# Moving the last pair of x's sums and two pooled differences by one step, and two bias copies to ScalarE, in a one-core hybrid decoder layer

## The chip, the core and the metric

The kernel runs on one core of one Trainium2 chip. The core has five engines, each with its own queue of instructions, which it works off in order: TensorE (PE; its weight loads are listed apart as PEld) multiplies matrices into PSUM banks, VectorE (DVE) and ScalarE (ACT) work element by element on SBUF tiles and PSUM banks, GpSimd (POOL) works on SBUF tiles, and SyncE (SP) issues most of the DMA transfers. The engines wait for each other by semaphores.

The metric is the time of one execution in microseconds (us), the median of several runs. The profile shows one more execution, instruction by instruction.

## The reference

One layer over 512 positions of width 1024, all in float32. Cut to what matters here:

```python
u = rmsnorm(x, ln1_g[i])
proj = u @ w_in[i]
q, k, v, pool_in, z, xbc, dt_raw, gate_pre = jnp.split(proj, split_idx, axis=-1)
y_a = dilated_attention_mixer(q, k, v, rel_bias) @ w_a[i]
y_b = pool_mixer(pool_in, pool_w[i], pool_scale[i]) @ w_b[i]
y_c = ssd_mixer(z, xbc, dt_raw, ...) @ w_c[i]
merged = gates[:, :, 0] * y_a + gates[:, :, 1] * y_b + gates[:, :, 2] * y_c
x = x + merged @ w_o[i]
x = x + conv_ffn(rmsnorm(x, ln2_g[i]), ...)
return rmsnorm(x, final_g)
```

Two of its parts matter for the change. The pool mixer takes, for each of four groups of 256 channels, the mean over the last w = 2, 4, 8 or 16 positions, less the channel itself:

```python
outs.append((c - shifted) / cnt - uf[..., sl])
```

The attention adds to its scores a bias, looked up in a table of 32 buckets per head by the distance of query and key.

## The kernel before

**Products in three parts.** A float32 product is computed from split operands. A weight block (a "job", with its own number n) is fetched into a tile raw, cast into a high part wh by ScalarE (`cast`, L200) and left with a low part wl = raw - wh by VectorE (`lows`, L220). `u` lies in SBUF, turned, as high part uh and low part ul. Each product is then high x high, high x low and low x high (`mm3`, L239), in this order, so that the low part wl is needed last. Buffers are few: two tiles wl, three wh, two raw. A low part can therefore only be written when TensorE has left the job two before it.

**Order of the jobs at the start.** Four jobs of pool channels (eight blocks m = 0 to 7 of 128 channels; the first two jobs are written out by hand in `begin`, L1872), then two jobs of v (n = 4 and 5, each with four row blocks, matmuls pb), then two sets of products for the first queries and keys, interleaved (n = 6 to 19, matmuls p), then the pool mixer's own product (n = 20, matmuls ppw). While job n is multiplied, the low part of n+1 and the cast of n+2 are issued ahead of its matmuls (`prepare`).

**Sets of seven.** Each set computes a 2 x 2 block product with seven products instead of eight (`sevens`), named one to seven. The operands are quarters of the weights and of u, or sums of such quarters. The weights' sums are made in place by `plus` (L354) on VectorE and by accumulating DMAs that GpSimd issues (L375). The sums of u are made by `sums_of_u(p)` for the pairs p = 0 to 3, as a generator in four stages, one a step: (A) two sums uf = uh + ul on VectorE (L390); (B) four half sums into sa and sb on VectorE (L329 to L332); (C) their high parts sah and sbh on ScalarE (L335, L336); (D) their low parts sal and sbl on VectorE (L338, L339). Job five (n = 8) is the first that reads them.

**Steps.** The side work runs in generators on a list `running`. After a certain number of matmuls the kernel calls `step()`, which advances every generator by one stage, in the order of the list. The steps that matter: steps 1 to 8 follow the pool blocks m = 0 to 7, steps 9 and 10 lie in v's first job (after two and after four row blocks), 11 and 12 in its second, and from 13 on there is one step after every second job of the sets (13 after n = 7, 14 after n = 9, 15 after n = 11, 16 after n = 13). `after(n, it)` waits n steps before the first stage. Line 1942 starts the pairs with waits of 0, 0, 5 and 6 steps. So pair 2 has its stages A to D in steps 6 to 9, pair 3 in steps 7 to 10.

**Pooling.** `pool_evac(m, ps)` (L956 on) copies block m out of its bank on ScalarE (pu, L963). GpSimd forms the running sums by doubling: one addition (L967) and one small copy (L968) for each shift 1, 2, 4, 8, each into a new tile psw, reading the one before, and at the end a correction of the first columns (L970). For m = 6 and 7 there are four such tiles each. The pooled difference is left to the generator `later()`, which waits a number of steps by m (L973) and then issues pd on VectorE (L976), its high part pdh on ScalarE (L978) and its low part pdl on VectorE (L979). m = 4 runs in step 8, m = 5 in step 9, m = 6 in step 12, m = 7 in step 15.

**Bias rows.** In step 9 `rows()` multiplies the bias table by a 0/1 matrix into two banks psr (L529) of 6 x 512 and 6 x 384, copies them into tiles rv on VectorE (L534), writes these to DRAM (L535) and reads them back, spread over partitions, into six tiles b0 to b5 (L542), which the attention uses from about 126 us on.

**v.** Each row block of v is copied out of its bank on ScalarE (L586), the first v group with 16 more columns, dtr (L588). The four banks that hold v's row blocks are those that the sets' products take next (`bank`, names c, a, b, y in order of their first use), the first product in the first block's bank.

**Slots.** Nearly all these tiles are made by `T()`, from a pool of 54 slots of 128 x 512 float32 with one tag. A tile that gets the slot of an earlier one waits until the last reader of that one is done. Within each of PE, ACT, DVE and POOL the instructions keep the order in which the program issues them.

Of the kernel before, what the change touches and what calls it, by code (L numbers as in the profile page):

```python
# [21 lines left out]
HEADS = 6  # L22
# [61 lines left out]
def trunk(ctx: ExitStack, tc, out, x, rel_bias, ln1_g, w_in, b_gate, w_a, pool_w, pool_scale, w_b,  # L84
# [3 lines left out]
    act, dve, pool, pe, sp = nc.scalar, nc.vector, nc.gpsimd, nc.tensor, nc.sync  # L88
# [19 lines left out]
    def T(name, dt=F32, shape=(P, S)):  # L108
        return big.tile(list(shape), dt, name=name, tag="t")
# [4 lines left out]
    def SM(name):  # L114
        return psum.tile([P, S], F32, name=name, tag="sm")
# [9 lines left out]
    waiting, running = [], []  # L125
# [38 lines left out]
    def after(n, it):  # L164
        for _ in range(n):
            yield
        yield from it
# [157 lines left out]
    def sums_of(f0, f1, ah, al, found, s=1):  # L325


        sa, sb = T("sa"), T("sb")
        dve.tensor_tensor(sa[:, LO], f0[:, HI], f1[:, HI], OP.add if s > 0 else OP.subtract)  # L329
        dve.tensor_tensor(sa[:, HI], sa[:, LO], f0[:, LO], OP.subtract)  # L330
        dve.tensor_tensor(sb[:, LO], f0[:, LO], f0[:, HI], OP.subtract)
        dve.tensor_tensor(sb[:, HI], f1[:, LO], sa[:, HI], OP.subtract if s > 0 else OP.add)  # L332
        yield
        bh, bl = T("sbh", F32R), T("sbl", F32R)
        act.copy(ah, sa)  # L335
        act.copy(bh, sb)  # L336
        yield
        dve.tensor_sub(al, sa, ah.bitcast(F32))  # L338
        dve.tensor_sub(bl, sb, bh.bitcast(F32))  # L339
        for j, h, l, half in ((1, ah, al, LO), (2, ah, al, HI), (3, bh, bl, LO), (4, bh, bl, HI)):  # L340
            found(j, h[:, half], l[:, half])
# [43 lines left out]
    def sums_of_u(p):  # L385

        f = []
        for k in (2 * p, 2 * p + 1):
            f.append(T("uf"))
            dve.tensor_tensor(f[-1], uh[:, k, :].bitcast(F32), ul[:, k, :].bitcast(F32), OP.add)  # L390
        yield
        yield from sums_of(*f, T("sah", F32R), T("sal", F32R),
                           lambda j, h, l: US.__setitem__((j, p), (h, l)), -1)
# [114 lines left out]
    def bias_rows():  # L508


        relb, hot = T("relb"), [T(f"hot{i}") for i in range(2)]
        dve.memset(relb[:, :18], 1.0)
        sp.dma_start(relb[:BUCKETS, :18], rel_bias)
        sp.dma_start(hot[0][:BUCKETS + 1, :S], c_hot[:, :S])
        sp.dma_start(hot[1][:BUCKETS + 1, :R_ALL - S], c_hot[:, S:])

        def part(tiles, lo, n):
            i = lo // S
            return tiles[i][:, lo - i * S:lo - i * S + n]

        def rows():
            rv = [T(f"rv{i}") for i in range(2)]
            rd = dram.tile([HEADS, R_ALL], F32, name="rdram")
            ps_r = [SM("psr0"), SM("psr1")]
            for g, (off, n) in enumerate(zip(R_OFF, R_LEN)):
                lo = off
                while lo < off + n:
                    m = min(off + n, (lo // S + 1) * S) - lo
                    pe.matmul(part(ps_r, lo, m)[:HEADS], relb[:BUCKETS + 1, 6 * g:6 * g + 6],  # L529
                              part(hot, lo, m)[:BUCKETS + 1], start=True, stop=True)  # L530
                    lo += m
            for i in range(2):
                m = (S, R_ALL - S)[i]
                dve.tensor_copy(rv[i][:HEADS, :m], ps_r[i][:HEADS, :m])  # L534
                sp.dma_start(rd[:, i * S:i * S + m], rv[i][:HEADS, :m])  # L535
            for i in range(6):
                b = T(f"b{i}")
                spans = ((0, 256, 0),) if i < 3 else ((1, P, 0), (2, P, 256))
                for g, width, at in spans:
                    src = bass.AP(tensor=rd.tensor, offset=rd.offset + R_OFF[g] + 2 * (i % 3) * R_ALL,  # L540
                                  ap=[[1, P], [R_ALL, 2], [1, width]])
                    sp.dma_start(b[:, at:at + 2 * width].rearrange("p (h c) -> p h c", h=2), src)  # L542
                bias.append(b)
            return
            yield

        return rows
# [411 lines left out]
    def pool_evac(m, ps):  # L959
        g = m // 2  # L960
        w = 2 << g
        u = T("pu")
        act.copy(u, ps)  # L963
        cur, sh = u, 1
        while sh < w:
            nxt = T("psw")
            pool.tensor_tensor(nxt[:, sh:], cur[:, sh:], cur[:, :S - sh], OP.add)  # L967
            pool.tensor_copy(nxt[:, :sh], cur[:, :sh])  # L968
            cur, sh = nxt, sh * 2
        pool.tensor_tensor(cur[:, :w], cur[:, :w], ramp[:, g, :w], OP.mult)  # L970

        def later():
            for _ in range((2, 2, 2, 2, 3, 3, 5, 7)[m]):  # L973
                yield
            d = T("pd")
            dve.scalar_tensor_tensor(d, cur, 1.0 / w, u, OP.mult, OP.subtract)  # L976
            dh, dl = T("pdh", F32R), T("pdl", F32R)
            act.copy(dh, d)  # L978
            dve.tensor_sub(dl, d, dh.bitcast(F32))  # L979
            DP[m] = (dh, dl)  # L980

        running.append(later())
# [880 lines left out]
    def begin(n, lo, hi, between=lambda early: None):  # L1863
        wh, wl = weights[n].split
        order = [(wh, uh, 0)]
        for k in range(1, KD):
            order += [(wh, uh, k), (wh, ul, k - 1)]
        order.append((wh, ul, KD - 1))
        for part in (order, [(wl, uh, k) for k in range(KD)]):
            for a, b, k in part:  # L1870
                for j in range(2):
                    pe.matmul(first[2 * n + j][:, lo:hi], a[:, k, j * P:(j + 1) * P], b[:, k, lo:hi],  # L1872
                              start=a is wh and b is uh and k == 0, stop=a is wl and k == KD - 1)
            between(part is order)
        if hi == S:
            for j in range(2):
                pool_evac(2 * n + j, first[2 * n + j])
                step()
# [60 lines left out]
            turned(k, 256, bank(k))  # L1939

    begin(1, 0, 256, turns)
    running.extend(after(n, sums_of_u(p)) for p, n in enumerate((0, 0, 5, 6)))
    turn()
    fetch(weights[2])
    fetch(weights[3])
# [8 lines left out]
    n = 0  # L1954
# [70 lines left out]
```

## Time and profile before

| | |
|---|---|
| median of 3 runs | 1025.43 us (1025.32 to 1025.86) |
| the profiled execution | 1025.91 us |
| its span, first instruction to last | 1024.1 us |
| granted TensorE clock, mean | 0.998 |
| DMA, mean over the span | 124 GB/s |

How to read the rows: a row of the timeline gives the start in us from the span's start, the duration in us, the engine, the line of the kernel, the operation, what it writes and reads, and how often it stands there in a row; in brackets stands the idle time of the engine before it and what ended that. Names of tiles are without their numbers, so all running sums are psw. Matmuls overlap at their ends, so the distance from start to start tells the pace of TensorE, not the duration.

### The profile page before, as it was taken

To read this page: it belongs to the slowest core of one execution; us is meant where nothing else is said; L and a number is where in the kernel's file an instruction comes from. 1 tells how busy PE (TensorE), PEld (TensorE's weight loads), DVE (VectorE), ACT (ScalarE), POOL (GpSimd) and SP (SyncE) were. 2 spreads that over 40 slices of the span, in tenths; PEclk is the share of its full clock that TensorE was granted. 3 is DMA by queue.
4 is the path that set the end of the run, shared out by engine and by line. 5 is a ranking of instruction groups with operands and counts; after the bars stand their busy time and mean duration, and the time that the engine had idled before them with its cause. 6 is when DMAs were issued, how large, how long until landed. Compare 5 with 4: busy or idle time off the path is not lost.

```text
span 1024.1 us, 14050 instructions
## 1 busy us (share of the span) xinstructions
PE 1013.5 (99%) x5504; PEld 865.9 (85%) x5504; DVE 738.2 (72%) x1022; ACT 502.6 (49%) x859; POOL 178.9 (17%) x147
## 2 busy tenths in 40 slices
PE   9999999999999999999999999999999999999997
PEld 9989878899998888888888888898888888888885
DVE  5787766777857758766758768867768677666775
ACT  6444655355545564567454335554454443443342
POOL 2592000001100004210144621102111101111120
PEclk9999999999999999999999999999999999999999
DMA  9326522147454244552253879342233224323142
GB/s 297 102 72 139 180 84 76 31 86 200 106 134 124 83 112 115 145 136 58 76 156 124 285 141 276 124 144 84 85 122 124 82 83 165 124 86 120 62 144 82
DMA packets 122129, 127.11 MB, mean 124 GB/s; under 512 B 5811, under 2 KB 103414, under 8 KB 122063
## 3 DMA queue, kind: packets, MB, share of 16 engines
q1 hardware_dynamic: 115999, 118.02, 36.6%
q0 software_dynamic: 5472, 7.34, 4.7%
q8 instruction: 43, 0.70, 0.3%
q10 hardware_dynamic: 592, 0.86, 0.2%
q14 instruction: 23, 0.19, 0.1%
HBM read 120.31 MB, written 2.22 MB: 120 GB/s over the span
## 4 chain that ended last, share of the span: by engine, by line
PE 93%; POOL 3%; DVE 2%; ACT 1%; issue 1%; POOLq 0%; DVEq 0%; ACTq 0%
PE pa L239 30%; PE p L239 23%; PE pu L239 22%; PE pqk L239 3%; PE pb L239 2%; PE pa L1872 2%; POOL psw L967 2%; PE ps L850 1%; PE pu L1640 1%; PE pt L878 1%; PE ppw L239 1%; PE po L891 1%; PE py L1176 1%; POOL psw L968 1%; PE pa L1829 1%
## 5 line engine op out<-in xcount | busy, mean ns | idle before, releaser
L220 DVE TENSOR_TENSOR wl<-raw,wh 128x2048 fp32r<-128x2048 f32 (+3 forms) x88 | 192.6, 2189 | 34.9 <-ACT wh L200 22.7
L200 ACT CAST wh<-raw 128x1024 fp32r<-128x1024 f32 (+3 forms) x174 | 166.8, 980 | 48.2 <-DVE raw L344 26.0
L1501 DVE SCALAR_TENSOR_TENSOR hc<-pu,fcol,hc 128x510 f32<-128x510 f32 x88 | 65.8, 748 | 60.7 <-ACT hc L1498 59.0
L239 PE MATMUL pa<-uh,wh 128*128 128x512 f32 x336 | 86.5, 399 | 0.0
L239 PE MATMUL pu<-uh,wl 128*128 128x512 f32 (+1 forms) x352 | 83.6, 380 | 0.0
L239 PE MATMUL pu<-uh,wh 128*128 128x512 f32 (+1 forms) x352 | 83.6, 379 | 0.0
L239 PE MATMUL pu<-ul,wh 128*128 128x512 f32 (+1 forms) x352 | 83.5, 379 | 0.0
L239 PE MATMUL pa<-ul,wh 128*128 128x512 f32 x336 | 83.0, 389 | 0.0
L239 PE MATMUL pa<-uh,wl 128*128 128x512 f32 x336 | 83.0, 389 | 0.0
L1506 POOL TENSOR_TENSOR hc<-hc 128x512 f32<-128x512 f32 x22 | 30.4, 1381 | 274.6 <-DVE hc L1501 240.1
L239 PEld LDWEIGHTS pu<-uh,wl 128*128 128x128 f32 x352 | 64.1, 188 | 12.8 <-DVE wl L220 0.3
L239 PEld LDWEIGHTS pu<-ul,wh 128*128 128x128 f32 x352 | 64.2, 188 | 12.5
L239 PEld LDWEIGHTS pu<-uh,wh 128*128 128x128 f32 x352 | 64.1, 188 | 12.4
L239 PEld LDWEIGHTS pa<-ul,wh 128*128 128x128 f32 x336 | 63.1, 188 | 13.3
L239 PEld LDWEIGHTS pa<-uh,wl 128*128 128x128 f32 x336 | 63.1, 188 | 13.1
L239 PEld LDWEIGHTS pa<-uh,wh 128*128 128x128 f32 x336 | 61.2, 188 | 12.8 <-issue 0.7
L1498 ACT ACTIVATE hc<-pu,fcol,fcol 128x512 f32<-128x512 f32 x40 | 31.2, 780 | 82.2 <-PE pu L239 81.9
L220 DVE TENSOR_TENSOR wl<-w,wh 128x1024 fp32r<-128x1024 f32 (+3 forms) x39 | 54.0, 1385 | 9.2 <-ACT wh L200 4.9
L200 ACT CAST wh<-w 128x512 fp32r<-128x512 f32 (+3 forms) x78 | 50.0, 684 | 21.0 <-DVE w L354 9.8
L375 POOL DMA_DIRECT2D w<-in_w_in_dram x14 | 17.2, 1231 | 189.6 <-DVE w L354 126.4
L871 ACT ACTIVATE sb<-sb,both 128x128 f32<-128x128 f32 (+1 forms) x72 | 30.1, 419 | 31.8 <-DVE both L868 21.7
L1503 ACT ACTIVATE hc<-hc 128x512 f32<-128x512 f32 x22 | 13.9, 632 | 42.9 <-DVE hc L1501 42.9
(400 smaller groups left out, 2027.3 us busy)
## 6 DMA issues: line engine op xcount, KB each, us to landing
raw<-in_ffn_w_up_dram SPq DMA_DIRECT2D x22, 1024.0 KB, 5.0
raw<-in_w_in_dram SPq DMA_DIRECT2D x21, 1024.0 KB, 5.1
raw<-in_ffn_w_down_dram SPq DMA_DIRECT2D x11, 1024.0 KB, 4.8
raw<-in_w_in_dram SPq DMA_DIRECT2D x16, 512.0 KB, 5.1
raw<-in_w_b_dram SPq DMA_DIRECT2D x4, 1024.0 KB, 4.8
al<-ad SPq DMA_DIRECT2D x16, 256.0 KB
raw<-in_w_c_dram SPq DMA_DIRECT2D x4, 1024.0 KB, 5.1
w<-in_ffn_w_down_dram SPq DMA_DIRECT2D x4, 1024.0 KB
```

Of the source, the lines that this page charges most:

```text
L200: act.copy(job.high[:, :, o], job.raw[:, :, o])
L220: (eng or dve).tensor_tensor(l[:, :, o], job.raw[:, :, o], h[:, :, o].bitcast(F32), OP.subtract)
L239: pe.matmul(ps, l, r, start=first and n == 0, stop=last and n == total - 1, skip_group_check=again)
L375: pool.dma_start(W[1][:, k:k + 2, at:at + n], src[:, k:k + 2, :], accum_op=OP.add)
L850: pe.matmul(pss[i][:, o:o + w * P], q[r, n * P:(n + 1) * P], k[r, kb * P:(kb + w) * P], start=True, stop=True)
L871: act.activation(sb[:, off:off + w * P], sb[:, off:off + w * P], AF.Exp, bias=nm[:, n, h:h + 1], accum_out=ls[:, n, h:h + 1])
L967: pool.tensor_tensor(nxt[:, sh:], cur[:, sh:], cur[:, :S - sh], OP.add)
L1498: act.activation(t, ps, AF.Identity, bias=ff["c1"][:, ff["b"] + m:ff["b"] + m + 1], scale=fw(2, m))
L1501: dve.scalar_tensor_tensor(t[:, sh:], ps[:, :S - sh], fw(k, m), t[:, sh:], OP.mult, OP.add)
L1503: act.activation(t, t, AF.Silu)
L1506: pool.tensor_tensor(a, a, t, OP.mult)
L1872: pe.matmul(first[2 * n + j][:, lo:hi], a[:, k, j * P:(j + 1) * P], b[:, k, lo:hi], start=a is wh and b is uh and k == 0, stop=a is wl and ...
```

## The change

```diff
-                dve.tensor_copy(rv[i][:HEADS, :m], ps_r[i][:HEADS, :m])
+                act.copy(rv[i][:HEADS, :m], ps_r[i][:HEADS, :m])
...
-            for _ in range((2, 2, 2, 2, 3, 3, 5, 7)[m]):
+            for _ in range((2, 2, 2, 2, 3, 3, 6, 8)[m]):
...
-    running.extend(after(n, sums_of_u(p)) for p, n in enumerate((0, 0, 5, 6)))
+    running.extend(after(n, sums_of_u(p)) for p, n in enumerate((0, 0, 5, 7)))
```

The two copies of the bias rows out of their banks are issued on ScalarE instead of VectorE, at the same place in the program. Pair 3 of u's sums has its stages A to D in steps 8 to 11 instead of 7 to 10. The pooled difference of m = 6 is issued in step 13 instead of 12, that of m = 7 in step 16 instead of 15. No operation is added or left out.

## The prediction

> **What bounds the kernel now.** Read first: the page's first parts, for which engine fills the span.
>
> ```profile
> span 1024.1 us, 14050 instructions
> PE 1013.5 (99%) x5504; PEld 865.9 (85%) x5504; DVE 738.2 (72%) x1022; ACT 502.6 (49%) x859; POOL 178.9 (17%) x147
> ```
>
> TensorE is busy 99% of the span, so work moved between the other engines counts only where TensorE waits for it. The three lines of the change act between 30 and 105 us, so the second view is the timeline there, TensorE first. The columns are start, duration, engine, line, operation, and in brackets the idle time with its releaser.
>
> ```profile
> 78.59 0.63 PE L239 MATMUL p<-uh,wh 128*128 128x256 f32 x4
> 79.06 0.64 PE L239 MATMUL p<-ul,wh 128*128 128x256 f32 x4
> 80.53 0.73 PE L239 MATMUL p<-uh,wl 128*128 128x256 f32 x4 [0.83 <-DVE wl L220]
> 81.10 0.64 PE L239 MATMUL p<-uh,wh 128*128 128x256 f32 x4
> ...
> 84.37 0.74 PE L239 MATMUL p<-uh,wl 128*128 128x256 f32 x4 [0.72 <-DVE wl L220]
> ...
> 86.23 0.74 PE L239 MATMUL p<-sah,wl 128*128 128x256 f32 x4 [0.18 <-DVE wl L220]
> 86.81 0.64 PE L239 MATMUL p<-sah,wh 128*128 128x256 f32 x4
> ```
>
> Groups of four follow each other every 0.48 us (79.06 - 78.59 = 0.47, with rounding). From the first p group to the one at 86.81 there are twelve intervals: 12 x 0.48 = 5.76 us were needed and 86.81 - 78.59 = 8.22 were taken. **2.46 us are lost**, all to low parts (wl) that VectorE delivers late. Why it is late stands in VectorE's own rows.
>
> ```profile
> 75.14 1.14 DVE L534 COPY rv<-psr 6x512 f32<-6x512 f32 x2
> 78.02 0.69 DVE L338 TENSOR_TENSOR sal<-sa,sah 128x512 fp32r<-128x512 f32 x1 [1.75 <-POOL psw L968]
> 78.63 0.71 DVE L339 TENSOR_TENSOR sbl<-sb,sbh 128x512 fp32r<-128x512 f32 x1
> 79.26 1.21 DVE L220 TENSOR_TENSOR wl<-w,wh 128x1024 fp32r<-128x1024 f32 x1
> 80.51 1.23 DVE L354 TENSOR_TENSOR w<-w 128x1024 f32<-128x1024 f32 x1
> 81.65 0.69 DVE L976 SCALAR_TENSOR_TENSOR pd<-psw,pu 128x512 f32<-128x512 f32 x1
> 83.02 0.69 DVE L979 TENSOR_TENSOR pdl<-pd,pdh 128x512 fp32r<-128x512 f32 x1 [0.69 <-ACT pdh L978]
> 83.63 0.68 DVE L220 TENSOR_TENSOR wl<-w,wh 128x512 fp32r<-128x512 f32 x1
> ```
>
> The first set's first low part stands behind the bias copies, a wait of 1.75 us for GpSimd, and the last pair's sal and sbl; the next low part stands behind the pooled difference of m=6. The wait is not one for data: sal is made of sa and sah, which GpSimd never touches. It is one for a slot. GpSimd's rows name the tile that held it.
>
> ```profile
> 73.30 1.37 POOL L967 TENSOR_TENSOR psw<-psw 128x510 f32<-128x510 f32 x1
> 74.61 0.64 POOL L968 COPY psw<-psw 128x2 f32<-128x2 f32 x1
> 75.34 1.03 POOL L967 TENSOR_TENSOR psw<-psw 128x508 f32<-128x508 f32 x1
> 76.31 0.19 POOL L968 COPY psw<-psw 128x4 f32<-128x4 f32 x1
> 76.58 1.27 POOL L967 TENSOR_TENSOR psw<-psw 128x504 f32<-128x504 f32 x1
> 77.80 0.19 POOL L968 COPY psw<-psw 128x8 f32<-128x8 f32 x1
> ```
>
> These are the running sums of m=7, each reading the tile before it. The copy of 128x8 ends at 77.99 and sal starts at 78.02, so sal took over the third running sum's slot. The first comes free after the 128x2 copy (75.25), the second after the 128x4 copy (76.50).
>
> **The change, part by part.** (Pairs of sums are numbered 0 to 3.) *Removed from VectorE ahead of the first low part:* the two bias copies (1.14), the slot wait (1.75), sal and sbl (0.61 + 0.63 from start to start). What moves later instead is told at its new place. The low part can start when pdl of m=5 is done. That moment hardly moves: the last pair's uf sums still start at 61.79, because no other VectorE instruction lies between the two steps, and its four half sums only change places with pd of m=4 and the two subtractions of pair 2, all of them still ahead of pd of m=5. I follow the order through with the lock told below and get pdl's end at 75.4 (before 75.22). So the first low part starts at about 75.3 instead of 79.26, and the 2.46 us of lateness are gone.
>
> *The copies on ScalarE.* No row shows ScalarE reading a 6-row bank.
>
> ```profile
> 73.80 0.62 ACT L978 CAST pdh<-pd 128x512 fp32r<-128x512 f32 x1 [3.40 <-DVE pd L976]
> 74.33 0.71 ACT L200 CAST wh<-w 128x256 fp32r<-128x256 f32 x2
> 74.94 0.47 ACT L586 COPY v<-pb 128x384 f32<-128x384 f32 x1
> 75.31 0.17 ACT L588 COPY dtr<-pb 128x16 f32<-128x16 f32 x1
> ```
>
> Bounds: 0.17 each (dtr, 16 columns) and 0.71 each (more than the v copy of 384 columns or a full cast of 512 took); I take 0.5, near the v copy, since the columns set it. They lie behind pdh, whose end I get at 74.6, so ScalarE goes on at 75.6. Hidden by the wait that follows; without it they would cost up to 1.4 in front of the v copies.
>
> *The slots.* Tiles of tag t get their slots in the order of first use, the slot longest free first; the tiles' addresses in the program of before show it, where b4, b5 and sal (pair 3) come one after another in that order and lie where m=7's first, second and third running sums lay, and sal's row bears it out. With the pair one step on, its sah and sbh come behind b5 instead of ahead of pd(m=5). So b4 and b5 get slots that have long been free, **sah takes the first, sbh the second, and the next tile in the order, the v tile of the first block of rows, the third**. sah, sbh and the v copies are ScalarE's, in this order, with the cast of the second set's weights between. A wait that stood on VectorE now stands on ScalarE. Queued behind it: all four v copies, and behind the first of those TensorE, since the first p group at 78.59 writes the bank that v copy and dtr empty.
>
> *When the third slot comes free.* VectorE, no longer idle from 76.28 to 78.02, now runs subtractions there, and these rows show what that does to GpSimd:
>
> ```profile
> 56.91 1.81 DVE L220 TENSOR_TENSOR wl<-raw,wh 128x1600 fp32r<-128x1600 f32 x1
> ```
>
> ```profile
> 57.12 2.50 POOL L967 TENSOR_TENSOR psw<-psw 128x510 f32<-128x510 f32 x1
> ```
>
> ```profile
> 58.65 1.25 DVE L329 TENSOR_TENSOR sa<-uf 128x256 f32<-128x256 f32 x1
> ...
> 61.79 2.13 DVE L390 TENSOR_TENSOR uf<-uh,ul 128x512 f32<-128x512 f32 x2
> 63.96 0.42 DVE L329 TENSOR_TENSOR sa<-uf 128x256 f32<-128x256 f32 x1
> ```
>
> GpSimd's sum takes 2.50 instead of 1.03: it ends 0.90 after wl does (58.72 to 59.62); and VectorE's next half sum, 0.42 when free, ends 0.28 after that. They take turns, one whole instruction each. The bias copies, in contrast, ran beside a sum of 1.03: they did not hold it up. By turns, from pdl's end at 75.4: copy 75.42; wl to 76.50; sum of 508 to 77.40; L354 to 78.50; copy 78.55 (second slot); sal to 79.10; sum of 504, 1.13 without its start, to 80.23; sbl to 80.78; copy **80.83 (third slot, before 77.99)**. ScalarE: sbh 78.6 to 79.2, cast to 79.9, v copy and dtr 80.85 to about 81.4. The first p group starts at 81.45, and restarting costs 0.09 (80.53 to 81.10 is 0.57 instead of 0.48). The group that stood at 86.81 stands at 81.45 + 0.09 + 5.76 = 87.30: **+0.5**. The later low parts have room: the second weights' by 81.5, needed at 85.4; the pooled pair of m=6 ends at 88.1 and the low part behind it at 89.3, needed at 89.7.
>
> The Trainium skill, SBUF — State Buffer, section "Who interferes with whom", has this as an exclusive lock: a VectorE instruction with two SBUF inputs and a GpSimd instruction that reads SBUF exclude each other for a whole instruction. By that rule the sum stays as above; if the two merely shared bandwidth, the result would lie near the first rival's.
>
> *The pooled difference of m=7, one step on.*
>
> ```profile
> 94.93 0.69 DVE L976 SCALAR_TENSOR_TENSOR pd<-psw,pu 128x512 f32<-128x512 f32 x1
> 96.30 0.69 DVE L979 TENSOR_TENSOR pdl<-pd,pdh 128x512 fp32r<-128x512 f32 x1 [0.69 <-ACT pdh L978]
> ...
> 98.11 1.22 DVE L220 TENSOR_TENSOR wl<-w,wh 128x1024 fp32r<-128x1024 f32 x1
> 99.37 1.22 DVE L354 TENSOR_TENSOR w<-w,raw 128x1024 f32<-128x1024 f32 x1
> ...
> 100.84 0.68 DVE L220 TENSOR_TENSOR wl<-w,wh 128x512 fp32r<-128x512 f32 x1
> ```
>
> The pair holds VectorE 1.98 us (94.93 to 96.91). Gone from there, it frees little: the next low part waits for its buffer until TensorE has left the one two sets back (about 95.7), the one after it until 97.15. So VectorE comes to the new place, ahead of the low part of 100.84, at 99.85, and that low part ends at 102.5 instead of 101.5. By the rhythm of 0.48 TensorE wants it at 102.2, and the low part behind it at 104.1, which gets it at 104.3. Two stalls of 0.46 and 0.36 with their restarts, less 0.19 saved at the low part of 98.11, give **+0.6**; bounds 0 and the whole 1.98.
>
> Sum: +0.5 + 0.6 = +1.1 us. The profiled execution took 1025.91 (span 1024.1 and 1.8 around it), 0.48 above the median of 1025.43; on the median this is **1026.5 us**, +0.1%.
>
> **The rivals.** *First, the stalls go and nothing takes their place:* either the v tile gets another slot, or GpSimd isn't held up, so that the third slot is free at 78.0 as now and the bank at 78.6. -2.46 + 0.6 gives 1023.6; with the pooled pair at nothing 1023.0. For it: three named stalls vanish whatever follows. Against it: the turns fit every row I followed from 57 to 75 us within 0.1.
>
> *Second, slower:* the m=7 pair lands ahead of the tightest low parts, and its whole 1.98 goes onto TensorE: +0.5 + 2.0, 1027.9. It decides from the point where the low part of 100.84 ends later than about 103.4 (each us behind 102.2 is one of TensorE's), so if ScalarE gives pdh a us late. Against it: in before ScalarE stands idle there ahead of its next copy.
>
> ```profile
> 101.66 0.60 ACT L774 ACTIVATE r<-p 128x512 f32<-128x512 f32 x1 [1.60 <-PE p L239]
> ```
>
> **How the numbers follow.** Forecast 0.60, first rival 0.26, second 0.14. A measurement of this kernel tells about 0.2%, 2 us, from no change. The first rival is half beyond that (1023.0 is, 1023.6 is not), the second wholly, the forecast (third slot 0.4 us earlier or later, m=7's pair between 0.2 and 1.1: 1025.7 to 1027.4) hardly: faster 0.15, within 0.2% 0.68, slower 0.17. The range reaches from 1023.2 to 1028.0.
>
> **What would show it.** Right: wl starts near 75.3; the sums of 508 and 504 take nearly 2 us each; sbh and the first v copy stand idle for GpSimd's psw, the copy starting near 80.9; the first p group waits nearly 3 us for ScalarE, and no p group before 88 for wl; two small wl stalls lie between 101 and 105. Wrong: the first p group starts near 78.6, or the v copy waits for TensorE alone; then the first rival holds.

## The result, and the profile after

| | before | after |
|---|---|---|
| median | 1025.46 us (1025.27 to 1026.06, 14 runs) | 1027.96 us (1026.61 to 1028.48, 14 runs) |
| the profiled execution | 1025.91 us | 1028.46 us |
| its span | 1024.1 us | 1026.7 us |
| first p group to first ppw group, in the trace | 78.59 to 111.48: 32.89 us | 81.36 to 114.12: 32.76 us |

The changed kernel is slower: ratio 1.0021, interval 1.0013 to 1.003. The time lies 2.5 us above before, where 1.1 was forecast, just inside the upper end of the range. From the first ppw group to the end of the span it is 912.62 us before and 912.58 after, so all of the difference lies ahead of that group. The first p group starts 2.77 us later, and the 32.76 us behind it are hardly shorter, though no p group waits for a low part before 104 us.

The busy times on the page of after do not say where the time went. TensorE's share is the same 99%, and its busy time is 1.2 us longer with as many matmuls as before.

```profile
PE 1014.7 (99%) x5504; PEld 867.5 (84%) x5504; DVE 738.6 (72%) x1020; ACT 503.9 (49%) x861; POOL 181.2 (18%) x147
```

The timeline of after, ScalarE and GpSimd first, then VectorE (columns as in the prediction):

```profile
74.42 0.94 ACT L534 COPY rv<-psr 6x512 f32<-6x512 f32 x2
...
78.49 0.62 ACT L336 CAST sbh<-sb 128x512 fp32r<-128x512 f32 x1 [2.49 <-POOL psw L968]
...
80.75 0.48 ACT L586 COPY v<-pb 128x384 f32<-128x384 f32 x1 [1.03 <-POOL psw L968]
...
75.43 1.90 POOL L967 TENSOR_TENSOR psw<-psw 128x508 f32<-128x508 f32 x1
77.28 1.18 POOL L968 COPY psw<-psw 128x4 f32<-128x4 f32 x1
78.54 1.58 POOL L967 TENSOR_TENSOR psw<-psw 128x504 f32<-128x504 f32 x1
80.07 0.65 POOL L968 COPY psw<-psw 128x8 f32<-128x8 f32 x1
...
75.23 1.21 DVE L220 TENSOR_TENSOR wl<-w,wh 128x1024 fp32r<-128x1024 f32 x1
76.48 1.94 DVE L354 TENSOR_TENSOR w<-w 128x1024 f32<-128x1024 f32 x1
```

The first low part is early (75.23 instead of 79.26). GpSimd's sums of 508 and 504 take 1.90 and 1.58 instead of 1.03 and 1.27, and ScalarE waits for their slots twice: sbh for the second, the v copy for the third, which comes free at 80.72 instead of 77.99. That is the chain of waits that the prediction laid out. TensorE's rows show what it did not lay out:

```profile
81.36 0.74 PE L239 MATMUL p<-uh,wh 128*128 128x256 f32 x4 [2.62 <-ACT dtr L588]
81.94 0.79 PE L239 MATMUL p<-ul,wh 128*128 128x256 f32 x4
82.53 1.06 PE L239 MATMUL p<-uh,wl 128*128 128x256 f32 x4
83.38 1.05 PE L239 MATMUL p<-uh,wh 128*128 128x256 f32 x4
84.24 1.05 PE L239 MATMUL p<-ul,wh 128*128 128x256 f32 x4
85.09 0.90 PE L239 MATMUL p<-uh,wl 128*128 128x256 f32 x4
85.83 0.64 PE L239 MATMUL p<-uh,wh 128*128 128x256 f32 x4
...
88.70 0.64 PE L239 MATMUL p<-sah,wh 128*128 128x256 f32 x4
```

No group in this stretch waits for anything after the first, yet they start 0.85 us apart between 82.53 and 85.09 instead of 0.48. The windows of after give the reason; behind the busy times of the engines stands PEclk, the granted clock as a share of full speed.

```profile
78.00:81.30 3.30, 0.74 (x5) 0.41 (x3) 3.15 (x4) 1.78 (x6) 3.14 (x4) 1.00 0.94 281
81.30:82.50 1.20, 1.14 (x8) 1.14 (x9) 0.69 (x1) 1.20 (x8) 1.13 (x2) 0.90 1.04 251
82.50:85.10 2.60, 2.60 (x15) 2.60 (x14) 0.00 (x0) 1.21 (x4) 0.29 (x1) 0.50 0.95 174
85.10:85.90 0.80, 0.80 (x6) 0.80 (x6) 0.00 (x0) 0.00 (x0) 0.00 (x0) 0.64 0.87 136
85.90:90.00 4.10, 4.10 (x36) 4.10 (x36) 2.93 (x4) 3.13 (x7) 1.24 (x1) 1.00 0.36 43
```

A busy time of 2.60 out of 2.60 at a clock of 0.50 looks like a fully used engine, but by the distances of 0.85 and 0.48 it does little more than half of the work (0.56). The means of 0.90 over 81.30 to 82.50 and of 0.64 over 85.10 to 85.90 put the low clock between 82.26 and 85.68. From the first p group to the thirteenth it is 7.34 us (81.36 to 88.70), against 8.22 with the three stalls of before and 5.76 at full pace. The late start cost 2.77 and the vanished stalls gave back only 0.88, which leaves **+1.89** at the thirteenth group (88.70 against 86.81).

The rest comes at the new place of m=7's pooled difference: between VectorE's instructions there, TensorE waits twice.

```profile
101.77 0.68 DVE L976 SCALAR_TENSOR_TENSOR pd<-psw,pu 128x512 f32<-128x512 f32 x1
...
103.75 0.69 DVE L220 TENSOR_TENSOR wl<-w,wh 128x512 fp32r<-128x512 f32 x1
...
104.49 0.74 PE L239 MATMUL p<-sah,wl 128*128 128x256 f32 x4 [0.27 <-DVE wl L220]
...
106.35 0.74 PE L239 MATMUL p<-sbh,wl 128*128 128x256 f32 x4 [0.16 <-DVE wl L220]
```

From the thirteenth group to the first ppw group before takes 24.67 us (86.81 to 111.48) and after 25.42 (88.70 to 114.12): **+0.75**. The two add up to 2.64; the spans differ by 2.6.

### The profile page after: what moved, and what is told of

It reads as the page before. It is cut to its first block, busy times and chain, and to the rows that moved or that the text cites. A ratio compares the mean times of both kernels' runs of the same rounds, so it can differ in the third digit from the quotient of the medians.

```text
span 1026.7 us, 14051 instructions
## 1 busy us (share of the span) xinstructions
PE 1014.7 (99%) x5504; PEld 867.5 (84%) x5504; DVE 738.6 (72%) x1020; ACT 503.9 (49%) x861; POOL 181.2 (18%) x147
## 3 DMA queue, kind: packets, MB, share of 16 engines
q0 software_dynamic: 5472, 7.34, 4.7%
## 4 chain that ended last, share of the span: by engine, by line
PE 93%; POOL 3%; DVE 2%; ACT 1%; issue 1%; POOLq 0%; DVEq 0%; ACTq 0%
PE pa L239 30%; PE p L239 23%; PE pu L239 22%; PE pqk L239 3%; PE pb L239 2%; PE pa L1872 2%; POOL psw L967 2%; PE ps L850 1%; PE pu L1640 1%; PE pt L878 1%; PE ppw L239 1%; PE po L891 1%; POOL psw L968 1%; PE py L1176 1%; PE pa L1829 1%
```

## The experiments

The theory has three parts: (1) the wait for the slots of m=7's sums moved to ScalarE and made TensorE idle; (2) that idle time made the clock fall, which cost some 1.4 us more; (3) m=7's pair at its new place cost 0.75. The rivals: the slow groups are a matter of data or weights and not of the clock; the slot is not what is waited for; the cost of m=7 lies elsewhere. All ratios are to the kernel before on the same chip, whose median there was 1025.8 to 1026.0, against 1025.46 beside the changed kernel. What a run gains on the changed kernel is therefore read from the traces.

**Filling the idle time.** After, with matmuls on ones into a bank that nobody reads, between v's last job and the first p group. They are work added, which the trace counts as twelve.

```diff
+        yield Call(lambda: keep_busy(FILL))
         for i, name in ((0, "one"), (1, "one"), (0, "five"),
+    def keep_busy(n):
+        ps = SM("fill")
+        for i in range(n):
+            pe.matmul(ps[:, :P], ones, ones, start=True, stop=True)
+FILL = 6
```

> The changed kernel with six small matmuls (ones by ones, 128 columns, into a bank that nobody reads) put on TensorE between v's second job and the first product of the sets, where it now idles 2.6 us. Theory (the idle time lets TensorE's granted clock fall to half, and the groups after 81.36 are slow for that reason): the first p group still starts near 81.4, since ScalarE's v copy still waits for the third slot, but the groups follow every 0.48 us at once, the granted clock stays at 1.00 from 81 to 86, and the time falls by 1.4 us to about 1026.5. Rival (the groups are slow because of the transfers or the weight loads at 81 to 86): pace and clock as now, 1028.

Measured: 1026.7 us (1026.34 to 1027.45, 11 runs), ratio 1.001 (1.0001 to 1.0019). The timeline of this kernel on TensorE, and a window of it behind the restart:

```profile
78.11 1.50 PE L1708 MATMUL fill<-ones 128*128 128x128 f32 x12
80.89 0.74 PE L239 MATMUL p<-uh,wh 128*128 128x256 f32 x4 [1.29 <-ACT dtr L588]
81.47 0.64 PE L239 MATMUL p<-ul,wh 128*128 128x256 f32 x4
81.95 0.64 PE L239 MATMUL p<-uh,wl 128*128 128x256 f32 x4
```

```profile
82.00:86.00 4.00, 4.00 (x35) 4.00 (x35) 1.83 (x2) 2.83 (x8) 0.32 (x1) 1.00 0.82 142
```

The wait for the slot is as long as in after; only the idle time is cut to 1.29 us. The clock stays at 1.00, and behind the restart (0.58) the groups run 0.48 apart at once. From the first p group to the thirteenth it is 5.86 us (80.89 to 86.75) instead of 7.34, and to the first ppw group 31.28 (to 112.17) instead of 32.76: 1.48 less. The median lies 0.9 above before there, where after lay 2.5 above. The weights, the data and the transfers are those of after, so this is shown: the fall of the clock is a cost of its own, and useless work in the gap removes it.

**Freeing the slot earlier.** After, with the first set's first sum of weights (the L354 of 76.48) on GpSimd, behind its sums, so that VectorE no longer takes turns with it there.

```diff
-            plus(W[0], W[1])
+            if plus_on:
+                plus_on.pop().tensor_tensor(W[0], W[0], W[1], OP.add)
+            else:
+                plus(W[0], W[1])
```

> The changed kernel with the one weight sum that follows the first low part (L354, 1.1 us on VectorE at 76.5) issued on GpSimd, behind its running sums, instead of VectorE. Theory (VectorE and GpSimd take turns, a whole instruction each, so that this sum holds the running sums up): GpSimd's third slot comes free at about 79.8 instead of 80.7, the first p group starts near 80.4, TensorE idles about 1.7 us, and if that is too short to lower the clock the time is about 1025.7, else 1027. Rival (GpSimd's running sums are slow there for another reason): third slot at 80.7 as now, 1028 or more.

Measured: 1027.31 us (1026.34 to 1027.73), ratio 1.0013 (1.0004 to 1.0022). Its timeline (its lines stand five further down) and two windows:

```profile
77.38 0.65 POOL L973 COPY psw<-psw 128x4 f32<-128x4 f32 x1
78.11 1.26 POOL L972 TENSOR_TENSOR psw<-psw 128x504 f32<-128x504 f32 x1
79.31 0.66 POOL L973 COPY psw<-psw 128x8 f32<-128x8 f32 x1
...
80.61 0.92 PE L239 MATMUL p<-uh,wh 128*128 128x256 f32 x4 [1.77 <-ACT dtr L593]
```

```profile
80.60:81.40 0.80, 0.79 (x5) 0.79 (x6) 0.65 (x1) 0.80 (x5) 0.80 (x1) 0.76 0.86 226
81.40:84.00 2.60, 2.60 (x14) 2.60 (x14) 0.00 (x0) 1.03 (x4) 2.27 (x2) 0.50 0.87 227
```

With one VectorE instruction less in the way the sum of 504 takes 1.26 again, the third slot is free 0.75 us earlier (79.97 against 80.72), and the first p group starts 0.75 earlier (80.61 against 81.36). So the slot is what is waited for, and the turns of the two engines set its time. The Trainium skill, SBUF — State Buffer, section "Who interferes with whom", calls this an exclusive lock; the row of 1.26 against 1.58 agrees. The clock fell all the same, after an idle time of 1.77 us: in this execution a shorter wait did not save that cost.

**Bias rows one job later.** After, with `rows()` in step 11 instead of 9, so that the b tiles come behind the pair in the order of slots and sah, sbh and the first v tile get slots long free.

```diff
-        yield Call(lambda: waiting.append(rows_of_bias()))
         for i, job in enumerate(v_jobs(0)):
             job.at_once = True
             yield job
             if i == 0:
+                yield Call(lambda: waiting.append(rows_of_bias()))
```

> The changed kernel with the bias rows issued two steps later (step 11 in place of 9), so that the tiles b0 to b2, which only DMA queues wait for, get the three slots of m=7's running sums, and sah, sbh and the first v tile get slots long free. Every engine has the same work. Theory (the loss is the slot wait on ScalarE and what follows from it): no wait for GpSimd in front of sbh and v, the first p group at 78.5 to 78.6 with pace 0.48 from the start; against the changed kernel -4.4 us, 1023.5. Rival (ScalarE or VectorE is simply fuller, or TensorE's bank is late for another reason): first p group still later than 80, 1027 to 1028.

Measured: 1025.1 us (1024.35 to 1028.84), ratio 0.9994 (0.9985 to 1.0003). The first p group starts at 78.28, nothing waits for psw, and the thirteenth group stands at 84.03, 5.75 later: full pace. That is the first half of the expectation. The time missed 1023.5, though, in part for a new reason:

```profile
88.91 1.24 POOL L375 DMA_DIRECT2D w<-in_w_in_dram  x1 [6.39 <-DMA b<-rdram]
...
103.23 0.41 ACT L200 CAST wh<-w 128x256 fp32r<-128x256 f32 x1 [3.26 <-DMA w<-in_w_in_dram]
...
104.27 0.74 PE L239 MATMUL p<-sbh,wh 128*128 128x256 f32 x4 [0.42 <-ACT wh L200]
```

By the profile's releaser GpSimd's second accumulating transfer of weights now goes out behind the nine b transfers (in before it went out at 87.47, in after at 86.58); why it has to wait for them isn't shown. The fourth, which completes the weights of the set, goes out at 99.56 instead of 96.28, its cast is late, and TensorE waits for wh; with the restart that is some 0.7 us. The rest of the miss is not accounted for. Beside this stand m=7's two stalls, as in after.

**m=7 back, and the parts alone.** After with m=7's pooled difference in step 15 as before:

```diff
-            for _ in range((2, 2, 2, 2, 3, 3, 6, 8)[m]):
+            for _ in range((2, 2, 2, 2, 3, 3, 6, 7)[m]):
```

> The changed kernel with the pooled difference of m=7 back in step 15 (7 instead of 8 steps), all else as changed. Theory (m=7's pair in step 16 stands ahead of the tightest low parts): the two stalls for wl at 104.5 and 106.4 go, one of 0.1 near 101 comes back, 0.75 us less, 1027.2. Rival (those stalls come from the late start of the sets): they stay, 1028.0.

Measured: 1027.4 us (1025.99 to 1028.84), ratio 1.0016 (1.0007 to 1.0024). In its trace both later stalls are gone, and the first p group to the first ppw group takes 32.02 us (81.08 to 113.10) instead of 32.76: 0.74 less. Part (3) of the theory holds.

Before with the pair of sums alone one step on, `enumerate((0, 0, 5, 7))`:

> The kernel before with only the last pair of sums one step on; the bias copies stay on VectorE, the pooled differences in steps 12 and 15. Theory: the slots are handed out as in the changed kernel, the bias copies (about 1 us, beside which GpSimd runs freely) stand ahead of the first low part, the third slot comes free near 80.3, the first p group starts near 80.9 and has no wl stall before 84: 1025.6 if the clock holds, up to 1027 where it falls. Rival (the pair's move frees VectorE and that is a gain): 1023 to 1024.5.

Measured: 1029.23 us (1028.02 to 1030.22, 6 runs), ratio 1.0033 (1.0021 to 1.0045), slower than I expected. The third slot came later still (81.97, in after 80.72):

```profile
75.41 1.14 DVE L534 COPY rv<-psr 6x512 f32<-6x512 f32 x2
76.48 1.20 DVE L220 TENSOR_TENSOR wl<-w,wh 128x1024 fp32r<-128x1024 f32 x1
...
75.61 2.96 POOL L967 TENSOR_TENSOR psw<-psw 128x508 f32<-128x508 f32 x1
...
82.61 0.74 PE L239 MATMUL p<-uh,wh 128*128 128x256 f32 x4 [3.68 <-ACT dtr L588]
```

The sum of 508 takes 2.96 us, until 0.89 after the low part's end, as the sum of 510 in before ended 0.90 after the low part beside it. So it looks as if it had been held up by the bias copies and then by the low part. In before a sum at the same distance behind the same copies took 1.03 and was not held up; why the copies blocked it here and not there stays open. The moved pair alone is thus the costliest single part; with the copies on ScalarE and m=6's pair later beside it (the run above) the time is 1027.4.

Before with the copies alone on ScalarE, `act.copy(rv[i][:HEADS, :m], ps_r[i][:HEADS, :m])`:

> The kernel before with only the two bias copies on ScalarE. Theory (sal waits for GpSimd's slot until 78.0 whatever VectorE does before): VectorE idles 1.1 us longer in front of sal, nothing else moves, 1025.4. Rival (the copies are part of the lateness of the low parts): 1.1 us less, 1024.3.

Measured: 1025.79 us (1025.12 to 1026.01), ratio 0.9999 (0.999 to 1.0008), with the stalls of before (0.84, 0.70, 0.16): without the moved pair VectorE waits for the slot instead of copying.

Before with the two pooled differences alone later, `(2, 2, 2, 2, 3, 3, 6, 8)[m]`:

> The kernel before with only the two pooled differences one step on. Theory: the first low part is as late as before (0.99 us and the restart), the second and the third are in time once m=6's pair is out of the way (-1.4 us), m=7's pair costs 0.75 us: 1024.8. Rival (m=6's move does nothing, since the pair only changes places with low parts that are late anyway): 1026.2.

Measured: 1025.49 us (1024.87 to 1026.78), ratio 0.9997 (0.9988 to 1.0005). The first stall (0.84) stays, the second and third go, and m=7's stalls of 0.27 and 0.17 appear; from the first p group to the first ppw group 32.27 us (78.79 to 111.06), 0.62 less than before. That is the 1.4 us of the two stalls less the 0.75 of m=7; the median moved by only 0.4.

**Towards a faster version.** The rows at step 11 with both pooled differences after six steps, `(2, 2, 2, 2, 3, 3, 6, 6)[m]`:

> The changed kernel with the bias rows two steps later, as in the run before last of the first four, and the pooled difference of m=7 in step 14, where VectorE waits about 2 us for TensorE, instead of 16. Theory: no stall at the start of the sets and none near 100 to 106: 1022.6, faster than both kernels by 2.8 and 5.3 us. Rival (VectorE's wait there isn't free, or the slots bring another wait): 1023.5 or more.

Measured: 1025.51 us (1024.05 to 1029.65), ratio 1.0001 (0.9991 to 1.0011). The profiled execution, the fastest, took 1024.05 and has one stall, 0.56 for wh. The four executions above 1026 had a mean granted clock of 0.995 or 0.996, the other seven 0.997 to 0.999, as if the clock had fallen in those four; none of them was traced, so this is not shown.

Before with the same steps and nothing else of the change:

```diff
-            for _ in range((2, 2, 2, 2, 3, 3, 5, 7)[m]):
+            for _ in range((2, 2, 2, 2, 3, 3, 6, 6)[m]):
```

> The kernel before with one edit: the pooled difference of m=6 one step later, as in the change, and that of m=7 one step earlier than before instead of one later. Theory (the low parts of the first sets wait for VectorE's order alone): the first low-part stall of 0.84 stays, the second and third go, as with m=6 and m=7 both later (1.38 us between the first p group and the 13th), and the two stalls of 0.27 and 0.17 behind 101 us go too, so the first ppw group starts near 109.7 (before 111.48 at a first p group of 78.59; with both later 110.3 to 110.5) and the time is 1.4 to 1.8 us below before, 1024.0 to 1024.5. Rival: m=7's pair lands one step earlier ahead of another tight low part, between 85 and 95 us, and gives the 0.75 of its later place back there: no difference from both later, 1025.5, with a new wl stall ahead of 95 us.

Measured: 1025.61 us (1024.96 to 1027.96), ratio 0.9999 (0.999 to 1.0008). Neither case came: m=7's stalls are gone, no wl stall lies ahead of 95 us but the first, and yet a stall of 0.94 for wh stands at 105.78; from the first p group to the first ppw group it is 32.63 us. GpSimd's and SyncE's rows in the timeline of this kernel, and then of before, name its origin:

```profile
92.50 1.20 POOL L375 DMA_DIRECT2D w<-in_w_in_dram  x1 [3.30 <-DVE wl L220]
92.90 0.37 SPq L188 DMA_DIRECT2D raw<-in_pool_w_dram  x1
101.12 1.24 POOL L375 DMA_DIRECT2D w<-in_w_in_dram  x1 [7.42 <-DMA raw<-in_pool_w_dram]
```

```profile
92.37 1.20 POOL L375 DMA_DIRECT2D w<-in_w_in_dram  x1 [3.66 <-issue]
93.81 0.37 SPq L188 DMA_DIRECT2D raw<-in_pool_w_dram  x1
96.28 1.24 POOL L375 DMA_DIRECT2D w<-in_w_in_dram  x1 [2.70 <-issue]
```

With the two stalls gone VectorE leaves the buffer raw 0.91 us earlier than in before, while GpSimd's third transfer goes out no earlier (92.50 against 92.37). SyncE sends the 1 MB fetch of pool_w at once, now ahead of the end of GpSimd's third issue (93.70) instead of behind it (93.57 before), and the fourth accumulating transfer goes out 4.8 us later. A buffer freed earlier cost most of what the vanished stalls had saved. The run with the two pooled differences alone shows the same pattern: fetch at 92.63, just behind the start of the third transfer (92.09), and the fourth only at 100.32. To test this, the kernel of (6, 6) with that fetch issued by ScalarE, in its own order behind the casts (`fetch` takes the engine as a new argument, left out here):

```diff
+                    if n == 14:
+                        fetch(weights[20], eng=act)
-                    if n + 3 < len(weights):
+                    if n + 3 < len(weights) and n != 17:
                         fetch(weights[n + 3])
```

> The kernel of the run before this one (m=6's pooled difference one step later, m=7's one earlier) with one more edit: the 1 MB fetch of pool_w is issued by ScalarE, in its own order behind the casts of about 97 us, instead of by SyncE as soon as its buffer is free (92.90). Theory: GpSimd's fourth accumulating transfer went out at 101.12 instead of 96.3 because that fetch had gone out ahead of it, while the third was being issued; with the fetch behind it the fourth goes out 2.7 us after the third has been issued, near 96.4, the stall of 0.94 for wh goes, and from the first p group to the first ppw group it is 31.6 to 31.8 us instead of 32.6 (before 32.89): 1024.5 to 1024.8. Rival: the fourth waits for something else (the third's own data, or the queue it shares with it); it stays near 101, the stall of 0.9 stays, and so does the time, 1025.6.

Measured: **1024.24 us** (1023.76 to 1024.83), ratio **0.9984** (0.9974 to 0.9993), faster than both kernels. In its timeline the fourth transfer is back in time:

```profile
91.62 1.21 POOL L375 DMA_DIRECT2D w<-in_w_in_dram  x1 [3.33 <-issue]
95.21 0.40 ACTq L188 DMA_DIRECT2D raw<-in_pool_w_dram  x1
96.22 1.24 POOL L375 DMA_DIRECT2D w<-in_w_in_dram  x1 [3.39 <-issue]
```

Between the first p group (77.99) and the first ppw group (109.34) lie 31.35 us instead of 32.89, with one stall left, the first low part's 0.86. Holding the fetch back decided. Whether it did so by the order of the two transfers, by the time between them or by the other queue, this run does not separate.

The same edit on the kernel with the rows at step 11 and (6, 6):

> The kernel with the bias rows at step 11 and m=6 and m=7 both after 6 steps, with the fetch of pool_w issued by ScalarE in the same way. Theory: the fourth accumulating transfer, at 98.93 there, goes out near 97.7, so that the one stall left (0.56 for wh) goes; the first accumulating transfer still waits for the b transfers. 0.5 below that kernel's profiled 1024.05: 1023.5 to 1023.7 for the fast ones of its runs. Rival, the fourth is late because the third is, or for its own data: 98.9 and a stall of 0.5 as before, 1024.0 and a median about 1025.5.

Measured: 1025.88 us (1024.89 to 1027.74), ratio 1.0 (0.9991 to 1.0009): a miss. The fourth transfer goes out at 97.77 as expected, but its data are late:

```profile
103.52 0.40 ACT L200 CAST wh<-w 128x256 fp32r<-128x256 f32 x1 [4.31 <-DMA w<-in_w_in_dram]
...
104.55 0.74 PE L239 MATMUL p<-sbh,wh 128*128 128x256 f32 x4 [1.73 <-ACT wh L200]
105.13 0.64 PE L239 MATMUL p<-sbl,wh 128*128 128x256 f32 x4
105.61 0.64 PE L239 MATMUL p<-sbh,wl 128*128 128x256 f32 x4
```

Both 1 MB fetches (94.30 and 96.83) are now under way when it starts, and the stall grew from 0.56 to 1.73. When a transfer goes out did not settle when its data came; that the two fetches held it up is argued from their times, not tested. One thing more stands in these rows: after 1.73 us of idle time the groups follow 0.48 apart, so here the clock did not fall, though it had fallen behind 1.77 in the run with the first sum of weights on GpSimd. The last section shows the difference.

## Why the prediction was right, and where it was not

- *The stalls on low parts go.* Right: wl of the first set starts at 75.23 (75.3 was given), and no p group before 88 waits for wl.
- *The slots go to sah, sbh and the v tile; GpSimd and VectorE take turns.* Right, within 0.11: sbh starts at 78.49 (78.6), the third slot is free at 80.72 (80.83), the v copy starts at 80.75 (80.85), the first p group at 81.36 (81.45). The sum of 504 took 1.58, as in the working and not the nearly 2 named among the signs. Freeing the slot 0.75 earlier moved that group by 0.75.
- *The copies on ScalarE are hidden.* Right. They took 0.94 together, where 0.5 each was taken.
- ***The term +0.5.*** Here the sum failed, in its size. It read: restarting costs 0.09 and then twelve intervals of 0.48 follow. Twelve intervals took 7.34 us instead of 5.85, and the term measured +1.89. The mechanism (a later start against vanished stalls) was right; what was missing is that behind 2.62 us without matmuls the granted clock fell to 0.50. The trace of before had no idle time there beyond 0.83 us, and 0.09 was carried over from such a gap to one three times as long. The one fall of the clock in that trace stands at its end, from 1020.73 on, nearly 4 us behind the last matmul; it could have told of such a cost, but not that 2.62 us were enough. The run with the gap filled came out 0.9 above before, where 1.1 was forecast.
- *m=7's pair, +0.6.* Right in its place and a little small: +0.75 by the two traces, 0.74 by putting it back. With their restarts, read from start to start, the two stalls cost 0.53 (103.58 to 105.07, less two intervals of 0.48) and 0.42 (105.55 to 106.93) instead of 0.46 and 0.36. Saved at the earlier low part were 0.20, where 0.19 was taken.
- *The rivals.* The first (1023.6, nothing takes the stalls' place) falls, since the slot did take their place. The second (m=7's whole 1.98) falls too: 0.75. The time landed next to its 1027.9, but by another mechanism.
- *The range and the chances.* The forecast's own bounds, 1025.7 to 1027.4, do not hold 1027.96; the whole range does, by 0.04, because it was stretched for the second rival, whose mechanism did not act. That is luck. The ratio of 1.0021 also lies a hair beyond the 0.2% that were held likeliest (0.68), on the side that was given 0.17.
- *The bias copies do not hold up a sum on GpSimd.* Read from one row of before; the run with the pair alone contradicts it (2.96), so it is no rule.

Of the 2.5 us, 1.9 are accounted for by the slot and the clock and 0.75 by m=7; the profiled pair differs by 2.6 in span. In the fourteen executions of after, three took 1026.61 to 1026.64 at a mean granted clock of 0.998 to 0.999, the others 1027.34 to 1028.48 at 0.997. A fall of 3.41 us to half lowers the mean by 0.0017, so that is what one would see if the clock did not fall in every execution. Only the profiled one was seen instruction by instruction.

## What to carry to other kernels

Price an idle stretch of TensorE by its length and not by the restart seen after a short one: here 1.77 us and more could cost 1.5 us on top, and whether they did depended on where the clock's grid cut them. Look at the granted clock in a narrow window behind it, since the mean of the run showed 0.997 and would not have told. Before moving instructions, write down which tile inherits which slot, for a moved tile passes its wait on to whichever engine comes next in that order. And when an engine gets faster, ask which transfers its buffers set free and what those overtake: the faster version here came from holding a fetch back.

## What the runs showed of the hardware

*The granted clock changed on a grid of 3.41 us, and what counted was the idle time within such a stretch.* In all four traces with a fall in the sets the low clock of 0.50 lasts 3.41 us, and the twelve intervals behind the gap take 7.33 to 7.36 us, with the gap filled 5.86. By the clock's records in the thirteen traces it first rises to 1.00 at 4.6 to 7.2 us. From there to the next change it is 75.09, 78.51, 1013.76 or 1017.17 us: 22, 23, 297 and 298 times 3.413. So these changes lie on a grid of 3.413 us that starts elsewhere in each execution. Counted from the first rise, TensorE's idle time in the stretches of this grid was:

| run | idle time, us | by stretch of the grid | clock behind it |
|---|---|---|---|
| m=7 back | 2.62 | 78.27 to 81.68: 2.62 | 0.50 |
| after | 2.62 | 78.85 to 82.26: 2.51 | 0.50 |
| the pair alone | 3.68 | 76.94 to 80.35: 1.43 | 1.00 |
| | | 80.35 to 83.77: 2.25 | 0.50 |
| first sum of weights on GpSimd | 1.77 | 77.59 to 81.01: 1.77 | 0.50 |
| rows at step 11, (6, 6), late fetch | 1.73 | 100.50 to 103.91: 1.09 | 1.00 |
| | | 103.91 to 107.33: 0.64 | 1.00 |
| gap filled | 1.29 | 76.68 to 80.09: 0.49 | 1.00 |
| | | 80.09 to 83.51: 0.80 | 1.00 |
| m=7 back, last matmul | to the end | 1016.94 to 1020.35: 1.88 | 1.00 |
| the pair alone, last matmul | to the end | 1019.02 to 1022.43: 2.40 | 0.50 |

The limit lies near half of a stretch. It is not sharp in these figures, as 1.77 brought a fall and 1.88 at the end of another trace did not; the ends of matmuls are modelled, and the clock may change somewhat behind the end of a stretch. That the idle time of 1.73 brought none fits, as the grid cuts it in two. If the grid lies anywhere with equal chance, both parts of the 2.62 us of after stay below the limit in 7% (limit 1.43) to 33% (limit 1.88) of the executions; this estimate from the table agrees with the three of fourteen that were shorter. The Trainium skill, TensorE: Matmul & The Clock Gate, Part 1 "The HAM clock gate", says that an idle window of about 3.4 us brings the clock to half and that as long a busy time brings it back, in windows that run freely. The half, the length and the free windows agree with these rows; that a window has to be idle throughout does not, as 1.77 us out of 3.41 did it here.

*GpSimd's next accumulating transfer went out about 4 us after the one before, and about 8 us when a 1 MB fetch had gone out on SyncE's queue just behind it.* From the start of the third to the start of the fourth it was 3.74 to 4.08 us in the seven traces in which the fetch of pool_w went out 1.44 us or more behind the third's start (before, 3.91, among them). It was 8.23 and 8.62 in the two in which the fetch followed it by 0.54 and 0.40 us (the pooled differences alone, and (6, 6)). With the fetch 2.7 us ahead of the third it was 5.09 and 5.79 (the two runs with the rows at step 11 and the fetch on SyncE's queue). With the fetch on ScalarE's queue it was 4.60, and 4.45 where that fetch went out 0.98 behind the third's start and still ahead of its end. So the order alone does not set it. Whether the fourth waits for the third's data, for room in its queue or for something else isn't shown.
